# A two-block fp32 network on one core: FFN groups loaded two ahead, gates one tile ahead, last sums of the layer norms on TensorE

## The chip, the cores and the metric

The kernel runs on one core of one Trainium2 chip. The metric is the device time of one execution in microseconds (us). The kernel before ran three times; its time is the median of the three. One further execution was taken by the hardware profiler, and every row shown below is from that one.

## What is computed

The input x has 1024 positions of 1024 channels, float32, and passes two blocks. Cut to what the change touches:

```python
def first_block(x, ...):
    x = x + mix @ w_out                      # mix: gated delta rule and spatial gating of rms_norm(x)
    h = rms_norm(x, norm_ffn)                # norm1
    ff = square(relu(h @ w_ff1))             # 1024 -> 4096
    x = x + ff @ w_ff2                       # 4096 -> 1024
    return rms_norm(x, norm_final)           # norm2
def second_block(x, ...):
    u, h, c_gate, b_gate, gate_a, gate_b = split(x @ w_in + b_in)
    y_a = glu(gelu(s5_ssm(u))) @ w_ssm_out   # S5: diagonal complex state, 32 groups
    y_b = (b_gate * conv(c_gate * h)) @ w_conv_out
    merged = sigmoid(gate_a) * y_a + sigmoid(gate_b) * y_b
    x = layer_norm(ALPHA * x + merged @ w_o, ln1_g, ln1_b)
    hid = silu(x @ w_gate) * (x @ w_up)      # 1024 -> 2816
    return layer_norm(ALPHA * x + hid @ w_down, ln2_g, ln2_b)
```

## The kernel before, in words

Channels lie on the 128 partitions and positions on the free axis, so an activation is eight tiles of 128x1024, each handled in two halves (`HS`) of 512 positions. Every fp32 operand of a product is split into a high and a low part (`split`, L342 to L344: ACT writes the high part, DVE or POOL subtracts it to get the low one), and a product is three passes, high times high, high times low and low times high (`mm`, L1316 to L1325). Weights come as pieces of 128x512 (256 KB): SP issues the load into one of three buffers `wr` (L620), then ACT writes `wh` and DVE or POOL `wl`.

**Order of work.** TensorE's order is the program's. The order on DVE, ACT, POOL and SP is set by a scheduler that simulates the program with estimated times; `K.late` keeps one instruction at its place in the program. Tiles come from pools that are opened and closed like a stack. `arena` opens one small pool for each numbered slot of 4 KB per partition, `sl` takes a tile in a slot, and a tile that reuses memory waits for the last readers of what lay there.

**Stages.** After `w_out` comes norm1 with `Forms` (L85 to L158): for the two big FFN products the kernel keeps seven combinations b11, b21, t1, t2, t3, t4, b22 of the activation's quarters, so that a unit (`sunit`, L1378) needs seven block products (`sprod`) where a direct form needs eight. `first` splits b11 and b21 as the tiles become final; `rest` makes the others, beginning with the four differences `ts` (t1, L125). `ffn1` runs 16 units, writes its 32 result tiles to DRAM (`ffd`), and reads them back in eight groups of four tiles (`load`, L1446); `unpack` splits a group into `fh` and `fl` (16 splits in two groups, 8 in one), and `down` multiplies it with `w_ff2` for the eight output tiles and adds to `res` (L1526). Between these products the generator `side` prepares the S5 tables (`s5_prep`): small DVE operations on 128x32 tiles, then four TensorE transposes (L1693). `arena()` (a local function of `mixers`) first closes the pools of ffn1's forms and opens the slots anew; only then are the S5 tiles taken.

In the second block, `merge` makes for each of eight output tiles two gate products (evacuated by a sigmoid), then the products with `w_conv_out` and `w_ssm_out`, and merges them. The merged tiles are split into `mh` and `ml`, `w_o` is multiplied (`wo`, `wo2`), and `ln_tail` makes the layer norm, first the sums of the first half (`N[0]`), then of the second (`N[1]`), which end under the first units of the second FFN. The layer norm (`Ln`) first subtracts a shift, the mean over the first four tiles (`shift_stat`, `shift_bc`, `sub`), then sums x and x*x tile by tile on DVE (`add`: L212 the sum `s`, L204 the sum `q` of the squares that ACT makes at L203) and adds over the 128 partitions with products of one column against ones (`colsums`, L1290; `stat`). The second FFN has 22 units, and `w_down` in five groups of tiles, read back like ffn1's; `ln2` is the last layer norm, and its end is the end of the program.

Of the kernel before, what the change touches and what calls it, by code (L numbers as in the profile page):

```python
# [16 lines left out]
P = 128  # L17
# [67 lines left out]
class Forms:  # L85
# [30 lines left out]
    def rest(self):  # L116
# [4 lines left out]
        for j, ((b11, b12), (b21, b22)) in enumerate(q):  # L121
            t = K.sl(self.slots["t4"] + j, "ts")
            t1, t2 = t[:, :HF], t[:, HF:]
            raw.append((t1, t2))
            V.tensor_tensor(t1, b12, b11, op=su)  # L125
            if self.gain:
                n.append(K.tmp("acc"))
                A.activation(n[j], b22, AF.Copy, scale=K.vec(self.gain, j + 4))
                V.scalar_tensor_tensor(t2, t1, self.neg[:, j:j + 1], n[j], op0=m, op1=ad)
            else:  # L130
                V.tensor_tensor(t2, b22, t1, op=su)
            self.split("t2", j, t2)
            yield
# [27 lines left out]
class Ln:  # L161
# [115 lines left out]
class Kern:  # L277
# [1176 lines left out]

    def finish(self, us, src, base):
# [9 lines left out]
        self.unpack(t)  # L1465
        for _ in u:
            pass
        return t

    def ffn1(self, F, res, sums, w0, arena):  # L1470
# [43 lines left out]
        for _ in rest:  # L1514
            pass
        ffs = [None] * 8
        base = (8, 16, 0, 8, 16, 0, 8, 16)
        ffs[0] = self.finish(us, ffd[:4], base[0])
        side = arena()
# [259 lines left out]
    def block2(self, y, N1, yd):  # L1779
# [172 lines left out]
        def sig(b, store):  # L1952
# [4 lines left out]
            return ev  # L1957
        for d in range(KD):
            for b, c in ((16, 2048), (24, 3072)):
                self.unit((W, c + d * P, y, sig(b, d)))  # L1960
            m = self.sl(mslot[d], "m")

            def evb(h, ps):
                V.tensor_tensor(m[:, self.HS[h]], ps, st["s", 24, h], op=M_)

            def eva(h, ps):
                t = st["s", 16, h]
                V.tensor_tensor(t, ps, t, op=M_)
# [4 lines left out]
        mg = [(self.sl(d, "mh", F32R), self.sl(8 + d, "ml", F32R)) for d in range(KD)]  # L1973
        for h in range(2):
            sl = self.HS[h]
            for d in range(KD):
                self.split(mg[d][0][:, sl], mg[d][1][:, sl], md[d][:, sl], (V, G)[d % 2])
        self.mark("wo")
        res = []
        for d in range(KD):  # L1980
            x = self.sl(100 + d, "res")
            dma(x, yd[d])
            res.append(x)
        def wo(d, hs):
            w = self.wts(I["w_o_2"], 0, d * P, KD)
            for h in hs:
# [16 lines left out]
        wl = []  # L2003
        for u in range(4):
            o = []
            for i in (12, 13) if u == 0 else (14, 15) if u == 1 else (2 * u + 4, 2 * u + 5):
                t = self.sl(X + i, "wx", F32R).rearrange("p (e t c) -> p e t c", e=2, t=4)
                o.append((t[:, 0], t[:, 1]))
            wl.append(self.left(I[("w_gate_2", "w_up_2")[u % 2]], u // 2 * 2 * P, o))
        self.ln_tail(N, wo, lambda d: self.wts(I["w_o_2"], 0, d * P, KD), wo2, pre, 2, 6)  # L2010
# [25 lines left out]
        for i in range(ahead):  # L2036
            next(us[i])
            next(us[i])
            for d in {1: (0, 1, 2, 3), 2: (4, 5, 6, 7)}.get(i, ()):
                n1.fin(d)  # L2040
            if i > 1:
                for _ in range(2):
# [3 lines left out]
        groups = [(0, 4), (4, 4), (8, 4), (12, 4), (16, 6)]  # L2046
        base = (X, 0, 8, X + 8, 0)

        def take(k, ts):
            for i, t in enumerate(ts):  # L2050
                hid[groups[k][0] + i] = t
        take(0, self.finish(us, hd[:4], base[0]))

        def down(f0, n, d, hs):
            w = self.wts(I["w_down_2"], f0 * P, d * P, n)
            for h in hs:
                sl = self.HS[h]
                ps = self.mm(w, [hid[f0 + k] for k in range(n)], sl)
                if f0 == 0:
# [3 lines left out]
        for k, (f0, n) in enumerate(groups[:-1]):  # L2063
            f1, m = groups[k + 1]
            ts = self.load(hd[f1:f1 + m], base[k + 1])
            self.unpack(ts)
            take(k + 1, ts)
            for d in range(KD):
                down(f0, n, d, (0, 1))
        self.mark("ln2")  # L2070
# [12 lines left out]
        def last(d, n, w, at):  # L2083
            sl = n.sl
            ps = self.mm(w, [hid[16 + k] for k in range(6)], sl, at)
            V.tensor_tensor(res[d][:, sl], ps, res[d][:, sl], op=Ad)
        N = self.ln_tail(N, lambda d, hs: down(16, 6, d, hs), wlast, last, pre2, 1, 4, True)
        N.stat()
        N.bc()
        for d in range(KD):  # L2090
            N.fin(d)

    def ln_tail(self, N, prod, wts, prod2, pre, ka, kb, cut=False):

# [11 lines left out]
        def bc(n):  # L2106
# [3 lines left out]
            for d in range(4):  # L2110
                n.sub(d)
        w = None
        parts = [N[0]]
        for k in range(2):
            if k == 1:
                parts.append(N[1])
            for d in range(4, KD):
# [5 lines left out]
                if k == 0:  # L2123
                    at = {4: {ka: stat, kb: lambda: bc(N[0])}, 5: {kb: lambda: bc(N[1])}}.get(d, {})
                else:
# [66 lines left out]
    def build(self):  # L2192
        tc, I = self.tc, self.I
        with ExitStack() as top:
# [12 lines left out]
            with tc.manual_schedule(engines={mybir.EngineType.PE}):  # L2207
                def arena():
                    self.fes.close()
                    self.arena(es, 8, 16)  # L2210
                    return self.s5_prep()
# [135 lines left out]
```

## Time and profile before

| | us |
|---|---|
| three runs: lowest, median, highest | 2880.91, 2884.34, 2886.09 |
| profiled execution, its own time | 2889.28 |
| its span in the profile | 2887.5 |
| TensorE (PE) busy | 2652.8 |
| DVE, POOL, ACT busy | 1569.5, 1092.4, 1005.8 |
| mean granted TensorE clock, share of 2.4 GHz | 0.952 |

The span runs from the first to the last instruction of the profile; the execution's own time has 1.8 us more, outside it, and lies 4.9 us over the median of the three runs. PEclk 1.00 is 2.4 GHz, 0.50 is 1.2 GHz. A row "[3.63 <-ACT fh L343]" says that the engine stood 3.63 us before this instruction and that the ACT instruction writing `fh` at line 343 released it. SPq rows are DMA issues. A row with x4 stands for four like instructions in a run.

### The profile page before, as it was taken

The page shows a single profiled execution, that of the slowest core. Times are in us where ns is not written, and L with a number is a line of the kernel's source. Part 1 is how long each engine was busy: PE and PEld are TensorE (multiplying, and loading weights), DVE is VectorE, ACT ScalarE, POOL GpSimd, SP SyncE. Part 2 cuts the span into 40 slices and gives each one's busy share as a digit, 9 for nine tenths or more (in the row PEclk, how much of TensorE's full clock was granted, in tenths as well). Part 3 has the DMA queues.
Part 4 walks back from the last instruction along what each step waited for, and adds up shares of the span by engine and source line. Part 5 has one row for each costly group of instructions (what it writes and reads, how often), then busy time and mean ns, then how long its engine had stood idle before and what let it go on. Part 6 is the DMA issues. An engine that isn't in the chain of part 4 may idle for free.

```text
span 2887.5 us, 39623 instructions
## 1 busy us (share of the span) xinstructions
PE 2652.8 (92%) x15032; PEld 2126.5 (74%) x15032; DVE 1569.5 (54%) x2585; ACT 1005.8 (35%) x1664; POOL 1092.4 (38%) x1041
## 2 busy tenths in 40 slices
PE   7776999799899999699999999999887999999996
PEld 5555676576678888588787887888666888888885
DVE  7799658864585545555554344100488444345337
ACT  4543442433354444212224224111244333343213
POOL 5765434332215331089804332333333433333220
PEclk9888998899989999899999999999998999999998
DMA  3332143221224334445425342111321322234311
GB/s 98 93 82 70 42 126 83 67 103 51 83 85 132 105 117 150 136 142 161 142 85 191 108 142 67 48 48 48 128 66 44 95 88 81 85 108 144 95 44 58
DMA packets 297118, 277.18 MB, mean 96 GB/s; under 512 B 26240, under 2 KB 248576, under 8 KB 296672
## 3 DMA queue, kind: packets, MB, share of 16 engines
q1 hardware_dynamic: 296928, 274.66, 30.8%
q8 instruction: 118, 1.93, 0.3%
q14 instruction: 72, 0.59, 0.1%
HBM read 210.23 MB, written 64.10 MB: 95 GB/s over the span
## 4 chain that ended last, share of the span: by engine, by line
PE 68%; DVE 18%; issue 4%; POOL 4%; DMA 3%; ACT 2%; SPq 1%; ACTq 0%; DVEq 0%; POOLq 0%
PE mm L1325 31%; PE mm L1376 24%; PE mm L636 5%; DVE stp L982 2%; DVE h L984 2%; PE wu L800 2%; DVE cy L789 1%; DMA fl<-ffd 1%; PE ob L800 1%; DVE acc L204 1%; DVE xl L424 1%; DVE fl L344 1%; PE cp L800 1%; DVE fbgkq L789 1%; DVE res L240 1%
## 5 line engine op out<-in xcount | busy, mean ns | idle before, releaser
L344 POOL TENSOR_TENSOR wl<-wr,wh 128x512 fp32r<-128x512 f32 (+1 forms) x261 | 346.0, 1326 | 855.2 <-ACT wh L343 772.7
L343 ACT ACTIVATE wh<-wr 128x512 fp32r<-128x512 f32 (+1 forms) x410 | 251.0, 614 | 801.1 <-PE mm L1325 460.4
L1376 PE MATMUL mm<-t,wh 128*128 128x512 f32 x1216 | 376.8, 391 | 9.8 <-DVE t L344 7.9
L1325 PE MATMUL mm<-fh,wh 128*128 128x512 f32 x816 | 321.5, 394 | 6.4 <-ACT fh L343 3.6
L1325 PE MATMUL mm<-fl,wh 128*128 128x512 f32 x816 | 320.1, 392 | 0.3 <-DVE fl L344 0.2
L1325 PE MATMUL mm<-fh,wl 128*128 128x512 f32 x816 | 319.3, 391 | 0.0
L1376 PEld LDWEIGHTS mm<-t,wh 128*128 128x128 f32 x1216 | 229.1, 189 | 59.1 <-DVE t L344 8.2
L1376 PE MATMUL mm<-b,wh 128*128 128x512 f32 x848 | 266.1, 394 | 6.0 <-DVE b L110 4.8
L1376 PE MATMUL mm<-t,wl 128*128 128x512 f32 x608 | 237.3, 390 | 0.0
L1325 PE MATMUL mm<-yh,wh 128*128 128x512 f32 x512 | 201.9, 394 | 0.0
L1325 PE MATMUL mm<-yl,wh 128*128 128x512 f32 x512 | 200.4, 391 | 1.0 <-DVE yl L344 1.0
L1325 PE MATMUL mm<-yh,wl 128*128 128x512 f32 x512 | 200.2, 391 | 0.0
L636 PE MATMUL mm<-xh,wh 128*128 128x512 f32 (+1 forms) x400 | 173.1, 433 | 24.4 <-ACT rows L851 7.2
L1376 PEld LDWEIGHTS mm<-b,wh 128*128 128x128 f32 x848 | 161.0, 190 | 42.5 <-DVE b L110 6.9
L1325 PEld LDWEIGHTS mm<-fh,wh 128*128 128x128 f32 x816 | 154.4, 189 | 41.4 <-ACT fh L343 7.8
L1407 POOL TENSOR_TENSOR ws<-wr 128x512 f32<-128x512 f32 x38 | 58.8, 1548 | 329.1 <-DVE wl L344 209.8
L344 DVE TENSOR_TENSOR wl<-wr,wh 128x512 fp32r<-128x512 f32 x149 | 110.6, 743 | 129.8 <-ACT wh L343 129.7
L1325 PEld LDWEIGHTS mm<-fl,wh 128*128 128x128 f32 x816 | 154.3, 189 | 33.8 <-DVE fl L344 2.0
L1325 PEld LDWEIGHTS mm<-fh,wl 128*128 128x128 f32 x816 | 154.4, 189 | 32.1
L636 PE MATMUL mm<-xl,wh 128*128 128x512 f32 (+1 forms) x400 | 171.2, 428 | 4.1 <-DVE xl L424 4.0
L344 DVE TENSOR_TENSOR wl<-ws,wh 128x512 fp32r<-128x512 f32 x152 | 113.4, 747 | 105.9 <-ACT wh L343 105.9
L636 PE MATMUL mm<-xh,wl 128*128 128x512 f32 (+1 forms) x400 | 169.6, 424 | 0.0
(504 smaller groups left out, 5448.6 us busy)
## 6 DMA issues: line engine op xcount, KB each, us to landing
wr<-in_w_in SPq DMA_DIRECT2D x112, 256.0 KB
wr<-in_w_ff SPq DMA_DIRECT2D x82, 256.0 KB
wr<-in_w_ff SPq DMA_DIRECT2D x32, 512.0 KB
fl<-ffd SPq DMA_DIRECT2D x32, 512.0 KB
wr<-in_w_gate SPq DMA_DIRECT2D x22, 512.0 KB
wr<-in_w_up SPq DMA_DIRECT2D x22, 512.0 KB
fl<-hd SPq DMA_DIRECT2D x22, 512.0 KB
wr<-in_w_down SPq DMA_DIRECT2D x40, 256.0 KB
```

The costliest lines, as they stand in the source:

```text
L204: K.V.tensor_tensor(self.q, self.q, t, op=ALU.add)
L240: K.V.tensor_tensor(r, r, self.rb, op=ALU.mult)
L343: self.A.activation(hi, src, AF.Copy)
L344: (lo_eng or self.V).tensor_tensor(lo, src, hi.bitcast(F32), op=ALU.subtract)
L636: self.T.matmul(ps, a[:, t, :], b[:, sl], start=(first and j == 0), stop=(last and j == 2))
L789: V.scalar_tensor_tensor(y[:, a:b], raw[:, a + o:b + o], cw[:, k:k + 1], y[:, a:b], op0=ALU.mult, op1=ALU.add)
L800: self.T.matmul(out(s), lhsT(s), rhs(s), start=start, stop=stop)
L982: V.tensor_tensor(tm, X3[:, :, 0:j, j:j + 1].to_broadcast([P, 2, j, n]), T3[:, :, j:j + 1, m:16].to_broadcast([P, 2, j, n]), op=ALU.mult)
L984: V.tensor_tensor(T3[:, :, 0:j, m:16], T3[:, :, 0:j, m:16], tm, op=ALU.subtract)
L1325: self.T.matmul(ps, a, b[:, sl], start=(start and k + j == 0), stop=(stop and k == n - 1 and j == 2))
L1376: self.T.matmul(ps, a[:, k, :], b, start=(start and k + j == 0), stop=(k == 3 and j == 2), skip_group_check=True)
L1407: G.tensor_tensor(s1, r21, r22, op=add)
```

## The change

It has six parts, each a change of order, of memory or of the engine that does a sum; what is computed stays the same.

1. `Forms.rest`: the difference t1 is kept at its place in the program (`K.late`).
2. ffn1: the slots of the forms are renumbered, so that the slots of FFN groups 0 and 1 (8 to 23) belong to an arena that stays open; only slots 24 to 27 and the pool `nf` are closed before the S5 preparation. `finish` loads groups 0 and 1, and the loop loads group g + 2.
3. merge: the gate products of tile d + 1 are put ahead of the products of tile d; the tiles 0 to 6 are split after the last gate product; the addition into m and all splits go to DVE (POOL made the low parts of every second tile before). Of the first `w_gate` and `w_up` pieces, one pair is now issued with each of the first four `w_o` tiles, where all four pairs stood ahead.
4. `Ln.add`: the last tile of eight gets no DVE addition; `stat` sums it on TensorE, 16 one-column products where 8 were.
5. Second FFN: groups two ahead, as in ffn1; the second half's `fin` in the order j, j + 4.
6. ln2: the products of group 3 for the output tiles 4 to 7 (`mid`) come after those of group 4 for tiles 0 to 3, and the shift of both halves is made among them.

```diff
@@ class Forms, rest
-            V.tensor_tensor(t1, b12, b11, op=su)
+            K.late(V.tensor_tensor(t1, b12, b11, op=su))
@@ class Ln, add
+        if d == KD - 1:
+            t = K.tmp("t")[:, :r.shape[-1]]
+            K.A.activation(t, r, AF.Square)
+            self.end = r, t
+            return
         self.sq(d)
@@ class Ln, stat
-        K.colsums(st[:, :n], self.s)
-        K.colsums(st[:, n:], self.q)
+        for e, xs in enumerate(zip((self.s, self.q), self.end)):
+            for i, x in enumerate(xs):
+                for k in range(n):
+                    K.T.matmul(st[:, e * n + k:e * n + k + 1], x[:, k * P:(k + 1) * P], K.ones[:, 0:1],
+                               start=e + i + k == 0, stop=i == 1, skip_group_check=True)
@@ finish
-        t = self.load(src, base)
+        ts = [self.load(*l) for l in loads]
@@ ffn1
-        ffs[0] = self.finish(us, ffd[:4], base[0])
+        src = [(ffd[4 * g:4 * g + 4], base[g]) for g in range(8)]
+        ffs = self.finish(us, src[:2])
         side = arena()
...
-            ffs[g + 1] = self.load(ffd[4 * g + 4:4 * g + 8], base[g + 1])
+            if g < 6:
+                ffs.append(self.load(*src[g + 2]))
@@ merge
-        for d in range(KD):
+        gates(0)
+        for d in range(KD):
+            if d + 1 < KD:
+                gates(d + 1)
+            else:
+                for e in range(KD - 1):
+                    part(e)
...
-                G.tensor_tensor(m[:, self.HS[h]], m[:, self.HS[h]], t, op=Ad)
+                V.tensor_tensor(m[:, self.HS[h]], m[:, self.HS[h]], ga[h], op=Ad)
...
-                self.split(mg[d][0][:, sl], mg[d][1][:, sl], md[d][:, sl], (V, G)[d % 2])
+        part(KD - 1)
@@ wo
+            ahead_w(d)
             w = self.wts(I["w_o_2"], 0, d * P, KD)
...
-        F = Forms(self, (X, X + 4, 4, 8, 0, X + 8, 12), res)
+        F = Forms(self, (X, X + 4, 0, 4, 8, X + 8, 12), res)
@@ ffn2, last groups
+        for k in range(4):
+            if k < 2:
+                ts.append(self.load(*src[k + 2]))
+            elif k == 2:
+                ts.append(self.load(hd[16:20], 0))
+            else:
+                ts[4] += self.load(hd[20:], 8)
+            self.unpack(ts[k + 1])
+            for d in range(KD if k < 3 else 4):
+                down(k, d, (0, 1))
@@ ln_tail
+        if mid:
+            for d in range(4, KD):
+                mid(d)
+                (stat, lambda: bc(N[0]), lambda: bc(N[1]), lambda: None)[d - 4]()
@@ mixers
-            self.arena(self.fes, 8, 20)
+            self.arena(es, 8, 16)
+            self.arena(self.fes, 24, 4)
...
-            F = Forms(self, (8, 12, 24, 20, 16, 4, 0), res, "norm_ffn")
+            F = Forms(self, (8, 12, 16, 20, 24, 4, 0), res, "norm_ffn")
```

**The order on DVE in norm1.** Rows are instructions in DVE's order, with their line. `b` is a form b11, b21 or b22, `ts` the raw difference t1, `res` the last addition of a product with `w_out`. Before:

```order
L2165 TENSOR_TENSOR res<-mm,res 128x512
L344 TENSOR_TENSOR wl<-wr,wh 128x512
L2165 TENSOR_TENSOR res<-mm,res 128x512
L125 TENSOR_TENSOR ts<-res 128x512 x2
L2187 TENSOR_TENSOR t<-t 128x512
L125 TENSOR_TENSOR ts<-res 128x512 x2
L344 TENSOR_TENSOR wl<-wr,wh 128x512
L110 SCALAR_TENSOR_TENSOR b_6958<-res,vecs,b_6958 128x512
L129 SCALAR_TENSOR_TENSOR ts<-ts,neg,acc 128x512
L110 SCALAR_TENSOR_TENSOR b_6994<-res,vecs,b_6994 128x512
L129 SCALAR_TENSOR_TENSOR ts<-ts,neg,acc 128x512
L110 SCALAR_TENSOR_TENSOR b_7032<-res,vecs,b_7032 128x512
```

And with the change, from the same last additions on:

```order
L110 SCALAR_TENSOR_TENSOR b_7211<-res,vecs,b_7211 128x512
L353 TENSOR_TENSOR wl<-wr,wh 128x512
L2194 TENSOR_TENSOR res<-mm,res 128x512
L353 TENSOR_TENSOR t_7618<-cb,t_7618 128x512
L353 TENSOR_TENSOR wl<-wr,wh 128x512
L2194 TENSOR_TENSOR res<-mm,res 128x512
L353 TENSOR_TENSOR wl<-wr,wh 128x512
L110 SCALAR_TENSOR_TENSOR b_7255<-res,vecs,b_7255 128x512
L2216 TENSOR_TENSOR t<-t 128x512 x2
L141 SCALAR_TENSOR_TENSOR cb<-res,neg,acc 128x512
L110 SCALAR_TENSOR_TENSOR b_7635<-res,vecs,b_7635 128x512
L353 TENSOR_TENSOR wl<-wr,wh 128x512
```

Before, the four differences stood ahead of eight splits of `b` (L110) that the first products read; with the change seven of these eight have gone ahead of the last addition, one (b_7255) is left behind it with one of b22, and the first difference comes eleven rows below the last one shown.

**The order on SP at the end of ffn1.** `ffd` numbers count the FFN's result tiles; in the rows of before 7285 is the first, so 7289 to 7292 are group 1 and 7297 the first of group 3. Before:

```order
L1483 DMA ffd_7315<-acc 128x512
L1483 DMA ffd_7316<-t 128x512
L620 DMA wr<-in_w_ff 128x4x128 x8
L1446 DMA fl<-ffd_7289 128x1024
L1446 DMA fl<-ffd_7290 128x1024
L1446 DMA fl<-ffd_7291 128x1024
L1446 DMA fl<-ffd_7292 128x1024
L1604 DMA s5t_9946<-in_s_b 128x512
L1604 DMA s5t_9947<-in_s_b 128x512
L1606 DMA s5t_9951<-in_c_i 16x16
L1606 DMA s5t_9952<-in_s_d 16x32
L1614 DMA d_m<-s5t_9955 4096x1x128
```

With the change 7288 is the first, so 7292 to 7295 are group 1 and 7296 to 7299 group 2:

```order
L1455 DMA fl<-ffd_7291 128x1024
L1455 DMA fl<-ffd_7292 128x1024
L629 DMA wr<-in_w_ff 128x4x128
L1455 DMA fl<-ffd_7293 128x1024
L1492 DMA ffd_7318<-t 128x512
L1455 DMA fl<-ffd_7294 128x1024
L1455 DMA fl<-ffd_7295 128x1024
L629 DMA wr<-in_w_ff 128x4x128
L1455 DMA fl<-ffd_7296 128x1024
L1455 DMA fl<-ffd_7297 128x1024
L1455 DMA fl<-ffd_7298 128x1024
L629 DMA wr<-in_w_ff 128x4x128
```

Group 1 has moved from behind eight pieces of `w_ff2` to just behind group 0; the S5 loads and the write of `d_m` now stand ahead of the last ten pieces that come before group 3.

**The order on SP at the product with `w_o`.** Before:

```order
L1982 DMA res<-yd_13049 128x1024
L1982 DMA res<-yd_13050 128x1024
L1982 DMA res<-yd_13051 128x1024
L620 DMA wr<-in_w_up 128x4x128
L620 DMA wr<-in_w_gate 128x4x128 x2
L620 DMA wr<-in_w_up 128x4x128 x2
L620 DMA wr<-in_w_o 128x4x128 x24
```

With the change:

```order
L629 DMA wr<-in_w_conv_out 128x4x128
L629 DMA wr<-in_w_ssm_out 128x4x128
L629 DMA wr<-in_w_gate 128x4x128 x2
L629 DMA wr<-in_w_o 128x4x128 x2
L629 DMA wr<-in_w_up 128x4x128 x2
L629 DMA wr<-in_w_o 128x4x128
L2003 DMA res<-yd_13045 128x1024
```

The first two pieces of `w_o` now stand behind one pair of `w_gate` pieces, where four pairs and the loads of `res` stood ahead of them.

## Rows read from the trace of the kernel before

**Rows 1.** page, part 1, PE: busy us (share of the span) xinstructions.

```profile
PE 2652.8 (92%) x15032; PEld 2126.5 (74%) x15032; DVE 1569.5 (54%) x2585; ACT 1005.8 (35%) x1664; POOL 1092.4 (38%) x1041
```

**Rows 2.** windows, columns: PE, PEld, DVE, ACT, POOL busy; PEclk; DMA share; GB/s.

```profile
1137.00:1182.00 45.00, 43.87 (x194) 36.01 (x192) 22.08 (x38) 9.98 (x18) 0.00 (x0) 1.00 0.30 97
1182.00:1211.10 29.10, 8.09 (x24) 4.90 (x24) 26.69 (x129) 11.79 (x22) 0.00 (x0) 0.68 0.75 257
2600.00:2830.00 230.00, 229.93 (x1019) 189.62 (x1018) 96.91 (x136) 51.30 (x92) 58.42 (x47) 1.00 0.27 87
```

**Rows 3.** timeline, PE, norm1; in brackets: idle before it and releaser.

```profile
819.61 0.79 PE L1376 MATMUL mm<-b,wh 128*128 128x512 f32 x1 [3.44 <-DVE b L110]
...
822.26 0.79 PE L1376 MATMUL mm<-b,wh 128*128 128x512 f32 x1 [1.01 <-DVE b L110]
```

**Rows 4.** timeline of DVE, norm1, beside it.

```profile
815.20 1.28 DVE L125 TENSOR_TENSOR ts<-res 128x512 f32<-128x512 f32 x2
...
817.01 1.28 DVE L125 TENSOR_TENSOR ts<-res 128x512 f32<-128x512 f32 x2
```

**Rows 5.** timeline, PE, ffn1 and S5 preparation.

```profile
1184.50 0.49 PE L1325 MATMUL mm<-fh,wh 128*128 128x512 f32 x1 [3.63 <-ACT fh L343]
...
1211.14 1.22 PE L1693 MATMUL mm<-ident,s5t 128*128 128x128 f32 x4 [18.22 <-DVE s5t L1686]
```

**Rows 6.** timeline of SP's queue, ffn1, DMA issues.

```profile
1142.21 34.94 SPq L620 DMA_DIRECT2D wr<-in_w_ff  x8
1180.22 1.76 SPq L1446 DMA_DIRECT2D fl<-ffd  x4
...
1185.09 8.91 SPq L620 DMA_DIRECT2D wr<-in_w_ff  x2
```

**Rows 7.** groups of DVE, 1182 to 1211 us, the largest.

```profile
L344 DVE TENSOR_TENSOR fl<-fl,fh 128x512 fp32r<-128x512 f32 x16 | 10.8, 683 | 0.6 <-ACT fh L343 0.6
```

**Rows 8.** timeline of PE, a later FFN group.

```profile
1421.17 0.66 PE L1325 MATMUL mm<-fh,wh 128*128 128x512 f32 x1 [2.81 <-DVE res L1526]
```

**Rows 9.** timeline of PE, the first product with w_o.

```profile
2052.39 0.80 PE L1325 MATMUL mm<-mh,wh 128*128 128x512 f32 x1 [14.00 <-ACT wh L343]
```

**Rows 10.** timeline of SP's queue before it.

```profile
2048.28 11.10 SPq L620 DMA_DIRECT2D wr<-in_w_o  x7
```

**Rows 11.** timeline, PE, first layer norm.

```profile
2133.46 3.54 PE L1290 MATMUL mm<-ones,acc 128*128 128x1 f32 x16 [5.12 <-DVE acc L212]
...
2169.70 1.84 PE L1290 MATMUL mm<-ones,acc 128*128 128x1 f32 x8 [7.79 <-DVE acc L212]
2174.16 1.86 PE L1290 MATMUL mm<-ones,acc 128*128 128x1 f32 x8 [2.62 <-DVE acc L204]
...
2212.12 0.80 PE L1376 MATMUL mm<-t,wh 128*128 128x512 f32 x1 [7.93 <-DVE t L344]
```

**Rows 12.** timeline, DVE, the first layer norm's last sums.

```profile
2166.00 1.75 DVE L204 TENSOR_TENSOR acc<-acc,t 128x512 f32<-128x512 f32 x1
...
2172.36 1.75 DVE L204 TENSOR_TENSOR acc<-acc,t 128x512 f32<-128x512 f32 x1
```

**Rows 13.** timeline of PE, last layer norm, the column sums.

```profile
2839.06 1.02 PE L1290 MATMUL mm<-ones,acc 128*128 128x1 f32 x8 [1.10 <-ACT t L203]
2841.76 1.86 PE L1290 MATMUL mm<-ones,acc 128*128 128x1 f32 x8 [1.68 <-DVE acc L204]
...
2864.11 2.68 PE L1290 MATMUL mm<-ones,acc 128*128 128x1 f32 x16 [3.48 <-DVE acc L212]
```

**Rows 14.** windows at low clock: PE busy, PEclk, DMA share, GB/s.

```profile
817.20:834.20 17.00, 13.24 (x37) 0.50 0.05 15
1196.20:1216.40 20.20, 5.26 (x14) 0.50 0.35 131
2042.60:2056.10 13.50, 3.58 (x8) 0.50 0.59 178
2841.30:2847.90 6.60, 6.14 (x19) 0.50 0.00 1
```

More of the change, by code (lines that the diff above doesn't have):

```diff
@@ L1453, in unpack, with finish @@
                 self.split(fh[:, sl], fl[:, sl], fl[:, sl].bitcast(F32))
-    def finish(self, us, src, base):
+    def finish(self, us, loads):
         for u in us[:-1]:
@@ L1462, in finish @@
         next(u); next(u)
-        t = self.load(src, base)
+        ts = [self.load(*l) for l in loads]
         next(u)
-        self.unpack(t)
+        self.unpack(ts[0])
         for _ in u:
             pass
-        return t
+        return ts
     def ffn1(self, F, res, sums, w0, arena):
@@ L1515, in ffn1 @@
             pass
-        ffs = [None] * 8
         base = (8, 16, 0, 8, 16, 0, 8, 16)
-        ffs[0] = self.finish(us, ffd[:4], base[0])
+        src = [(ffd[4 * g:4 * g + 4], base[g]) for g in range(8)]
+        ffs = self.finish(us, src[:2])
         side = arena()
@@ L1957, in sig, with gates, part @@
             return ev
-        for d in range(KD):
+        def gates(d):
             for b, c in ((16, 2048), (24, 3072)):
                 self.unit((W, c + d * P, y, sig(b, d)))
+            st["g", d] = [[st["s", b, h] for h in range(2)] for b in (16, 24)]
+        def part(d):
+            sl = self.HS
+            mg.append((self.sl(d, "mh", F32R), self.sl(8 + d, "ml", F32R)))
+            for h in range(2):
+                self.split(mg[d][0][:, sl[h]], mg[d][1][:, sl[h]], md[d][:, sl[h]])
+        mg = []
+        gates(0)
[5 more added lines that the diff above has]
+                    part(e)
             m = self.sl(mslot[d], "m")
+            ga, gb = st["g", d]
             def evb(h, ps):
-                V.tensor_tensor(m[:, self.HS[h]], ps, st["s", 24, h], op=M_)
+                V.tensor_tensor(m[:, self.HS[h]], ps, gb[h], op=M_)
             def eva(h, ps):
-                t = st["s", 16, h]
-                V.tensor_tensor(t, ps, t, op=M_)
-                G.tensor_tensor(m[:, self.HS[h]], m[:, self.HS[h]], t, op=Ad)
+                V.tensor_tensor(ga[h], ps, ga[h], op=M_)
+                V.tensor_tensor(m[:, self.HS[h]], m[:, self.HS[h]], ga[h], op=Ad)
             self.unit((I["w_conv_out_2"], d * P, bz, evb))
@@ L1972, in block2 @@
             md.append(m)
[L1973 to L1976, printed above, removed]
-                self.split(mg[d][0][:, sl], mg[d][1][:, sl], md[d][:, sl], (V, G)[d % 2])
+        part(KD - 1)
         self.mark("wo")
@@ L1983, in block2, with ahead_w @@
             res.append(x)
+        wl = []
+        def ahead_w(u):
+            o = []
+            for i in (12, 13) if u == 0 else (14, 15) if u == 1 else (2 * u + 4, 2 * u + 5):
+                t = self.sl(X + i, "wx", F32R).rearrange("p (e t c) -> p e t c", e=2, t=4)
+                o.append((t[:, 0], t[:, 1]))
+            wl.append(self.left(I[("w_gate_2", "w_up_2")[u % 2]], u // 2 * 2 * P, o))
         def wo(d, hs):
+            ahead_w(d)
             w = self.wts(I["w_o_2"], 0, d * P, KD)
@@ L1998, in block2 @@
         N = [Ln(self, res, h, "ln1_g", "ln1_b") for h in range(2)]
-        F = Forms(self, (X, X + 4, 4, 8, 0, X + 8, 12), res)
+        F = Forms(self, (X, X + 4, 0, 4, 8, X + 8, 12), res)
         for n in N:
             n.out = F
[L2003 to L2009, printed above, removed]
         self.ln_tail(N, wo, lambda d: self.wts(I["w_o_2"], 0, d * P, KD), wo2, pre, 2, 6)
@@ L2038, in block2 @@
             next(us[i])
-            for d in {1: (0, 1, 2, 3), 2: (4, 5, 6, 7)}.get(i, ()):
-                n1.fin(d)
-            if i > 1:
+            for j in {1: (0, 1), 2: (2, 3)}.get(i, ()):
+                n1.fin(j)
+                n1.fin(j + 4)
+                next(rest)
+            if i > 2:
                 for _ in range(2):
@@ L2047, in block2, with down @@
         base = (X, 0, 8, X + 8, 0)
[L2049 to L2055, printed above, removed]
+        src = [(hd[f:f + n], b) for (f, n), b in zip(groups, base)]
+        ts = self.finish(us, src[:2])
+        def down(k, d, hs, w=None, at={}):
+            f0, n = groups[k]
+            w = w or self.wts(I["w_down_2"], f0 * P, d * P, n)
             for h in hs:
                 sl = self.HS[h]
-                ps = self.mm(w, [hid[f0 + k] for k in range(n)], sl)
-                if f0 == 0:
+                ps = self.mm(w, ts[k], sl, at)
+                if k == 0:
                     V.scalar_tensor_tensor(res[d][:, sl], res[d][:, sl], ALPHA, ps, op0=M_, op1=Ad)
@@ L2062, in down @@
                     V.tensor_tensor(res[d][:, sl], ps, res[d][:, sl], op=Ad)
[L2063 to L2069, printed above, removed]
+        for k in range(4):
[8 more added lines that the diff above has]
+                down(k, d, (0, 1))
         self.mark("ln2")
@@ L2081, in wlast, with ln_tail @@
             return [(hi[:, t, :], lo[:, t, :]) for t in range(6)]
[L2083 to L2089, printed above, removed]
+        n = self.ln_tail(N, lambda d, hs: down(4, d, hs), wlast, lambda d, n, w, at: down(4, d, (n.h,), w, at), pre2, 1, 4,
+                         True, lambda d: down(3, d, (0, 1)))
+        n.stat()
+        n.bc()
         for d in range(KD):
-            N.fin(d)
-    def ln_tail(self, N, prod, wts, prod2, pre, ka, kb, cut=False):
+            n.fin(d)
+    def ln_tail(self, N, prod, wts, prod2, pre, ka, kb, cut=False, mid=None):
         for d in range(4):
@@ L2123, in ln_tail @@
                 if k == 0:
-                    at = {4: {ka: stat, kb: lambda: bc(N[0])}, 5: {kb: lambda: bc(N[1])}}.get(d, {})
+                    at = {} if mid else {4: {ka: stat, kb: lambda: bc(N[0])}, 5: {kb: lambda: bc(N[1])}}.get(d, {})
                 else:
@@ L2209, in arena @@
                     self.fes.close()
-                    self.arena(es, 8, 16)
                     return self.s5_prep()
```

## The prediction

> **What bounds the kernel now.** I read the page first. TensorE (PE) is busy 92% of the span [rows 1], so a gain can only come from the remaining gaps or from faster multiplying. The windows then show where there are gaps: none in the second FFN's last groups, where PE is busy for 229.93 of 230 us at the full clock [rows 2], but 8.09 of 29.10 us busy between 1182 and 1211 us. The timeline of PE gives each gap its length and releaser; after 800 us nearly all of it lies in six places: norm1 [rows 3], ffn1 with the S5 preparation [rows 5], a later FFN group [rows 8], the first product with `w_o` [rows 9], and the two layer norms [rows 11, 13]. Last come the windows at low clock: behind most waits PEclk is 0.50, the 1.2 GHz level [rows 14]. At 2.4 GHz a matmul of 512 columns takes 229.93/1019 = 0.226 us [rows 2]; at the low level the 37 in 13.24 us, 16 of them one-column sums, and the 14 in 5.26 us give 0.36 to 0.38 [rows 14], partly because short gaps and cheap ones lie among them. I charge 0.20 us for each 512-column matmul at the low level, from 0.226 to about 0.43, twice 0.226. A wait thus costs its length and this surcharge.
>
> **Norm1.** The reader is to see what DVE does while PE waits: four differences, 1.28 us for two and again 1.28 us for two [rows 4], ahead of the splits of `b` that release PE after 3.44 and 1.01 us [rows 3]. The order with the change has seven of the eight splits ahead of the last addition. Waits of 4.45 us go, and with them 21 wide matmuls at the low level, 37 less 16 sums, 21 x 0.20 = 4.2 us [rows 14]; together 8.6 us. What is late next: the lows of t2, now behind the differences. I count 45 DVE operations of 0.68 us and 12 small ones of 0.16 between the last addition and the last t2, 32.5 us, while PE has 120 wide matmuls (27.1 us), 16 sums and 4 broadcasts, some 31 us. That is a draw, and a new wait may be 0 to 4 us, with a surcharge as much again at worst. Bounds: 0.6 to 8.6. I take **6**, nearer the upper end, as the scheduler puts the t2 it can wherever DVE is free.
>
> **ffn1 and S5.** PE waits 3.63 us for the first high part of group 1 and 18.22 us for the S5 tables [rows 5]. SP shows why: eight `w_ff2` pieces go out one by one from 1142.21, and only at 1180.22 group 1 and then the S5 loads [rows 6]; all wait for the old pools, which PE reads until then. With the change group 1 stands just behind group 0, and the S5 tiles wait only for slots 24 to 27 and `nf`, last used by ffn1's last unit, which is over when the pieces of group 0's products are issued from 1142.21 on. DVE then has to hide the tables. In the 29.10 us of the wait it is busy 26.69 [rows 2], 10.8 of it splits of two groups [rows 7], so the tables are at most 15.9 us, or 13 without four other wide operations of 0.68. In 1137 to 1182 us DVE is busy 22.08 of 45 us [rows 2], which leaves 22.9; until PE reaches the transposes, 24 matmuls later, another 5.4. The load is 13 to 15.9 and 5.4 for the eight splits of group 1: 18.4 to 21.3 of 28.3 us. It fits by 7 us, if small operations don't queue badly. The write of `d_m` holds SP: the two weight pieces behind it take 8.91 us to issue [rows 6]. With the change eight pieces stand there that are issued 3 to 4 products ahead of use (5.44 us each, 24 matmuls), so 16 us or more cover it; were that cover gone, 8.9 us would show once. The gain: 3.63 + 18.22, plus 14 matmuls at the low level [rows 14], four of them transposes (some 2.4): 24.3 at most; 8 if the tables end 16 us later than needed, all of DVE's 15.9. I take **23**, near the upper end, as the count leaves 7 us.
>
> **The later group.** The 2.81 us at 1421 [rows 8] come of DVE standing behind splits whose loads were issued late; a group earlier they are on chip. Bounds 0 and 2.81 plus 1.6, if eight matmuls follow at the low level as behind `w_o`, 4.4. I take **3**. In the second FFN the same edit has nothing to hide [rows 2]: 0.
>
> **Merge and `w_o`.** PE waits 14.00 us for the first high part of `w_o` [rows 9], whose load is issued only at 2048.28 [rows 10], 9.9 us after PE stopped (2052.39 - 14.00 = 2038.39), behind the four pairs. With the change two pieces of `w_o` stand behind one pair, and the last gate product comes 21.8 us (96 matmuls) earlier, so that twelve splits of tiles 0 to 5 run under the last two products. Only tile 7's chain (an addition, a split, about 2.8 us at 0.68 each) is left, and it is wanted as the last of eight in a 5.44 us product. POOL's additions move to DVE: 16 x 0.68 = 11 us over eight tiles, beside PE at 100%. The gain: 14.00 and 8 matmuls at the low level (1.6) [rows 14] = 15.6 at most; at least 2, if the buffers come free only at PE's end, as before. I take **15**.
>
> **Column sums.** Each of four sums loses two DVE additions and gets 16 rows more (8 products; the profile shows two rows for each). The 16 rows take 3.54 us in the first layer norm [rows 11] and 2.68 in the last [rows 13], 8 rows 1.02 at best: 0.13 to 0.22 us a row, 2.0 to 3.5 us for 16. The Trainium skill ("TensorE: Matmul & The Clock Gate", section "Back-to-back issue gap") puts a floor of about 25 ns under the start of one matmul to the next however few its columns. By that floor, an estimate, 16 rows would take 0.4 us and the four sums together gain some 8 us more than I forecast; the trace does not agree, with 0.13 us at best, and I go by the rows.
> - First layer norm, first half: the wait of 5.12 ends with L212 [rows 11]. The sums of tile 6 end some 2 us before those of tile 7, and 16 more rows take 2.0 to 3.5 of it back: -1 to +2.5, I take **1**.
> - Second half: the waits of 7.79 and 2.62 [rows 11] end with tile 7's two sums. With the change the last DVE addition is tile 6's, which ends at 2167.75, against 2174.11 for tile 7's [rows 12]. Sixteen rows of `q` at the low level follow, 3.6 us: end 2171.4, where the sums now end at 2176.0. Gain **4.6**; 1.7 if the three weight splits slip in, 6 if the clock stays up. The 7.93 us at 2212 [rows 11] stay: DVE is what PE waits for there, and the order leaves 42 of the 43 operations ahead of that split.
> - Last layer norm, first half: 1.10 + 1.68 [rows 13], and 11 wide matmuls at the low level, 19 less 8 sums (2.2) [rows 14], with the shift's 16 DVE operations now under group 3's products. Less 2.0 for the rows: 0 to 5, I take **3**.
> - Its second half ends the program: two additions less (1.4), 16 rows more (2.0 to 3.5), of which `s` can run earlier: -2 to +1, **0**.
>
> **The sum.** 6 + 23 + 3 + 15 + 1 + 4.6 + 3 = 55.6 us from the profiled execution's own 2889.28: 2833.7. That execution lies 4.9 us over the median of the three runs; taken at the same distance the median is 2828.8, so **2829**. All upper bounds together are 67.4 us, median 2817; all lower ones about 9, median 2875.
>
> **Rivals.**
> 1. *The S5 tables are still late.* DVE is in order, and the 109 small operations (129 less 16 splits and four others) wait for each other and stand between evacuations. For it: DVE had 26.69 of 29.10 us of work there [rows 2]. Against it: 7 us to spare. If half the wait stays, 9 us and its surcharge 3 go back: 2841.
> 2. *`w_o` is still late.* The `w_gate` pieces are split into slots that the merge's last products may hold, and ACT would stand there ahead of `w_o`. For it: the order on SP still has one pair ahead of `w_o`. Against it: the first pair lies where tiles 4 and 5 were, which are split 20 us earlier. It costs 14: 2843.
> 3. *Group 1 and S5 wait for the pools as before*, that is, the change does not do what it says. Then 23 and part of the 3 are lost: 2853. Against it: the order on SP, and that the arena for slots 8 to 23 is open from the start.
> 4. *Slower.* In ffn1's down products SP carries 4 MB of groups and the 2 MB of `d_m` at once with 256 KB pieces of `w_ff2`. If pieces came late in each of the 64 products from there on, PE would wait once per product and fall to 1.2 GHz behind each wait, as behind the waits of [rows 14]. It decides from 55.6/64 = 0.9 us per product; at 1.2 us the time is 2829 + 77 = 2906. Against it: PE is at 43.87 of 45 us and the DMA share is 0.30 in 1137 to 1182 [rows 2], and half the traffic would still fit.
>
> **Chances.** Forecast, all parts within their bounds: 0.66. Rival 1: 0.12; rival 2: 0.09; rival 3: 0.06; rival 4: 0.03; several small new waits, time within 0.2% of before, 0.04. A measurement can tell about 0.2%, 6 us. Faster: 0.66 + 0.12 + 0.09 + 0.06 = 0.93; same 0.04; slower 0.03. The range of 2813 to 2857 takes in rivals 1 to 3; it leaves out rival 4 and the 0.04 above, and some 0.10 of forecast and rivals at either edge, where bounds add up.
>
> **What would show it.** Right: SP issues group 1 before 1135 us; no wait over 2 us before the transposes; `w_o` loads before the merge's end and PE without a gap there; at low clock no window after 1140 to 1540; 32 rows in each sum. Norm1 wrong: a wait for `t` at L1385 near 845 us. Rival 1: a wait for `s5t`; rival 2: ACT waiting ahead of `wx`. The forecast is wrong if new waits of over 20 us stand where none were, above all on DVE in 1140 to 1190 us.

## The result, and the profile after

The changed kernel takes 2832.64 us (median of 4 runs, 2831.41 to 2834.16) where before takes 2885.22 (median of 4 runs as well, one more than ahead of the prediction; 2880.91 to 2887.94): a ratio of 0.9819, 95% interval 0.9802 to 0.9836. The forecast was 2829 in 2813 to 2857.

PE's row of the page, part 1, of the kernel after:

```profile
PE 2649.6 (94%) x15096; PEld 2126.8 (75%) x15096; DVE 1576.1 (56%) x2601; ACT 1006.6 (36%) x1664; POOL 1074.6 (38%) x1017
```

Against [rows 1], PE works as long as before (2652.8) in a span that is 57.1 us shorter (2887.5 to 2830.4): waits went, not work. The second view is the windows of ffn1 and the S5 preparation after, columns as in [rows 2]:

```profile
1137.00:1182.00 45.00, 45.00 (x200) 37.28 (x199) 39.90 (x157) 13.32 (x27) 0.00 (x0) 1.00 0.59 182
1182.00:1211.10 29.10, 29.10 (x136) 24.26 (x135) 15.85 (x25) 9.00 (x21) 6.83 (x9) 1.00 0.38 116
```

DVE now does in 1137 to 1182 what it did in the wait: 39.90 us busy against 22.08, PE has no gap, and PEclk is 1.00 in both windows.

Since PE runs the same products in both kernels, but for the sums, I read the trace at eight of them and compare the stretches between (us; the product that ends a stretch is the same in both, and the last stretch ends with ACT's last instruction):

| stretch | before | after | less by | forecast |
|---|---|---|---|---|
| start to the last product with `w_out` | 814.2 | 814.4 | -0.2 | 0 |
| norm1 and the 16 units of ffn1 | 323.0 | 321.2 | 1.8 | 6 |
| first down products, S5 tables | 83.9 | 56.2 | 27.7 | 23 |
| later groups | 301.7 | 301.8 | -0.1 | 3 |
| norm2, u, conv, S5 | 228.1 | 227.4 | 0.7 | 0 |
| glu, merge, first product with `w_o` | 312.1 | 292.8 | 19.3 | 15 |
| first layer norm, first half | 79.8 | 77.4 | 2.4 | 1 |
| second half, units of the second FFN | 470.9 | 466.9 | 4.0 | 4.6 |
| its down products, last layer norm, end | 270.6 | 269.2 | 1.4 | 3 |

The waits that are left, from the timeline of PE after (norm1, a later group, the two layer norms):

```profile
852.27 0.80 PE L1385 MATMUL mm<-t,wh 128*128 128x512 f32 x1 [3.31 <-DVE t L353]
...
856.88 0.79 PE L1385 MATMUL mm<-t,wh 128*128 128x512 f32 x1 [2.96 <-DVE t L353]
...
1382.78 0.50 PE L1334 MATMUL mm<-fh,wh 128*128 128x512 f32 x1 [1.80 <-DVE res L1535]
...
2080.81 1.05 PE L227 MATMUL mm<-ones,res 128*128 128x1 f32 x8 [0.69 <-DVE res L2026]
2082.49 1.05 PE L227 MATMUL mm<-ones,acc 128*128 128x1 f32 x8 [0.63 <-DVE acc L204]
...
2111.01 1.02 PE L227 MATMUL mm<-ones,acc 128*128 128x1 f32 x8 [0.97 <-DVE acc L218]
...
2115.94 1.87 PE L227 MATMUL mm<-ones,acc 128*128 128x1 f32 x8 [3.01 <-DVE acc L204]
...
2154.88 0.79 PE L1385 MATMUL mm<-t,wh 128*128 128x512 f32 x1 [6.37 <-DVE t L353]
...
2804.92 1.05 PE L227 MATMUL mm<-ones,acc 128*128 128x1 f32 x8 [2.27 <-DVE acc L218]
2805.84 1.03 PE L227 MATMUL mm<-ones,res 128*128 128x1 f32 x8
2806.73 1.44 PE L227 MATMUL mm<-ones,acc 128*128 128x1 f32 x8
2808.03 1.85 PE L227 MATMUL mm<-ones,t 128*128 128x1 f32 x8
```

The waits before the b products [rows 3], before the transposes [rows 5] and before `w_o` [rows 9] have no successor. Two are new, 3.31 and 2.96 us before t2 in norm1. The sums of the first layer norm begin after 0.69 and 0.97 us where they waited 5.12 and 7.79 [rows 11], but now PE stands 3.01 us inside them; the 32 rows at the end of the program take 4.96 us (2804.92 to 2809.88), where 16 took 2.68 [rows 13].

### The profile page after: what moved, and what is told of

Read it like the earlier page. It is cut to its first block, busy times and chain, and to the rows that moved or that the text cites. A ratio compares the mean times of both kernels' runs of the same rounds, so it can differ in the third digit from the quotient of the medians.

```text
span 2830.4 us, 39715 instructions
## 1 busy us (share of the span) xinstructions
PE 2649.6 (94%) x15096; PEld 2126.8 (75%) x15096; DVE 1576.1 (56%) x2601; ACT 1006.6 (36%) x1664; POOL 1074.6 (38%) x1017
## 4 chain that ended last, share of the span: by engine, by line
PE 75%; DVE 17%; issue 3%; DMA 2%; ACT 2%; POOL 1%; SPq 0%; ACTq 0%; POOLq 0%; DVEq 0%
PE mm L1334 38%; PE mm L1385 25%; PE mm L645 5%; DVE h L993 2%; DVE stp L991 2%; PE wu L809 2%; DVE cy L798 1%; DVE fbgkq L798 1%; DVE xl L433 1%; DVE res L249 1%; PE ob L809 1%; PE gram L809 1%; PE cp L809 1%; PE mm L227 1%; DMA ca<-rd 0%
## 5 line engine op out<-in xcount | busy, mean ns | idle before, releaser
L353 POOL TENSOR_TENSOR wl<-wr,wh 128x512 fp32r<-128x512 f32 (+1 forms) x261 | 352.6, 1352 | 871.9 <-ACT wh L352 781.9
L1416 POOL TENSOR_TENSOR ws<-wr 128x512 f32<-128x512 f32 x38 | 65.1, 1712 | 316.3 <-DVE wl L353 216.3
```

What stands on the lines that cost most here:

```text
L353: (lo_eng or self.V).tensor_tensor(lo, src, hi.bitcast(F32), op=ALU.subtract)
L1416: G.tensor_tensor(s1, r21, r22, op=add)
```

## The experiments

Each kernel is the changed one with one edit (`slots_old` and `ws_dve2` have two, `best` three), timed beside the kernel before on the same chip, and profiled once. The part ahead of norm1, which no edit touches, took 809.3 to 817.0 us in these profiles, so medians of neighbours a few us apart don't decide; the stretches do. They scatter too: over the changed kernel and those whose edit lies elsewhere, norm1 with its units took 318.9 to 321.5 us, the later groups 300.4 to 302.4, glu, merge and the first product with `w_o` 292.4 to 296.3, the first half of the first layer norm 77.4 to 79.7, its second half with the units 464.5 to 466.9, the end 268.5 to 270.9. Only what lies outside these is read as an effect.

**What freed the S5 tables: memory or the order of the loads?** Two kernels. In the first, loads go back to one group ahead in the program, slots as changed:

```diff
-        ffs = self.finish(us, src[:2])
+        ffs = self.finish(us, src[:1])
-            if g < 6:
-                ffs.append(self.load(*src[g + 2]))
+            ffs.append(self.load(*src[g + 1]))
```

> The slots stay as changed, but ffn1 loads its groups one ahead, as before. Theory: the S5 preparation waited for memory, so the freed slots alone remove the wait of 18 us before the transposes; group 1 is issued a little later but no longer behind a pool, at most 4 us come back: 2833 to 2837. Rival: it is the early issue of group 1 that counts; then PE waits some 4 us for its high part and the splits push the S5 tables behind the transposes again: 2845 to 2860.

Measured: 2829.77 us, ratio to before 0.9801 (0.9786 to 0.9815); the S5 stretch 56.2 us, as after. SP's queue, DMA issues, of this kernel:

```profile
1114.37 0.32 SPq L1455 DMA_DIRECT2D fl<-ffd  x1
...
1115.73 4.40 SPq L1455 DMA_DIRECT2D fl<-ffd  x4
...
1122.11 0.43 SPq L1455 DMA_DIRECT2D fl<-ffd  x1
...
1123.55 0.84 SPq L1455 DMA_DIRECT2D fl<-ffd  x2
...
1126.59 3.04 SPq L1455 DMA_DIRECT2D fl<-ffd  x3
...
1130.67 0.32 SPq L1455 DMA_DIRECT2D fl<-ffd  x1
```

These are twelve group loads, three groups, before 1131 us, in the same order as after: the scheduler issues a load when its slot is free, wherever it stands in the program. The rival falls, and of the theory's 4 us at most nothing came back: loading two ahead is worth nothing here. In the second, the slots go back too:

```diff
-            self.arena(es, 8, 16)
-            self.arena(self.fes, 24, 4)
+            self.arena(self.fes, 8, 20)
-            F = Forms(self, (8, 12, 16, 20, 24, 4, 0), res, "norm_ffn")
+            F = Forms(self, (8, 12, 24, 20, 16, 4, 0), res, "norm_ffn")
...
+                    self.arena(es, 8, 16)
```

> ffn1 as before (old slots, groups one ahead), all else as changed. Theory: the freed slots alone carry the S5 gain, so the waits of 3.6 and 18.2 us and the low clock behind them are back, 27.6 us from the first down product to behind the transposes: 2857 to 2860. Rival: part of the S5 gain came of the other parts (other order on DVE and SP): under 20 us.

Measured: 2861.76 us, ratio 0.9913 (0.9897 to 0.9930); the S5 stretch is 83.4 us, 27.2 more than after. PE's timeline has the old waits again:

```profile
1183.86 0.80 PE L1334 MATMUL mm<-fh,wh 128*128 128x512 f32 x1 [3.61 <-ACT fh L352]
...
1211.04 1.22 PE L1702 MATMUL mm<-ident,s5t 128*128 128x128 f32 x4 [17.72 <-DVE s5t L1695]
```

The theory holds: the memory carries the whole gain, and rival 3's mechanism is what the edit brings back. (Norm1, whose forms lie in their old slots again in this kernel, takes 324.7 us, 3.5 more than after; that is a second loss and not part of the 27.2.)

**What freed `w_o`: SP's order or the gates?** In one kernel the gate products go back to just ahead of their tile:

```diff
-        gates(0)
         for d in range(KD):
-            if d + 1 < KD:
-                gates(d + 1)
-            else:
+            gates(d)
+            if d + 1 == KD:
                 for e in range(KD - 1):
                     part(e)
```

> Gate products in the old order (tile d just ahead of its own products), splits of tiles 0 to 6 after the last gate product and w_o pieces between the pairs as changed. Theory: the place of the w_o pieces on SP is what removed the 14 us; the splits still have the last two products of 10.9 us as cover, so 0 to 1 us comes back: 2833. Rival: the cover by the gate product moved ahead is needed, tile 6 or the weights are late: 2838 to 2847.

Measured: 2829.34 us, ratio 0.9801 (0.9782 to 0.9820), the merge stretch 292.9 us against 292.8. In the other the four pairs stand ahead of `w_o`:

```diff
+        for u in range(4):
+            ahead_w(u)
         def wo(d, hs):
-            ahead_w(d)
```

> Gates one tile ahead as changed, but all four pairs of w_gate and w_up pieces ahead of w_o, as before. Theory (SP's order decides): the w_o load is again issued behind pieces whose buffers come free only when the merge ends, PE stands 10 to 14 us before the first product with w_o and runs on at the low clock: 2844 to 2849. Rival: with the gates ahead the three buffers turn over early enough and nothing comes back: 2833.

Measured: 2838.27 us, ratio 0.9842 (0.9821 to 0.9862), the merge stretch 304.0, 11.2 more. PE's timeline in this kernel:

```profile
2009.47 0.79 PE L1334 MATMUL mm<-mh,wh 128*128 128x512 f32 x1 [8.15 <-ACT wh L352]
```

And SP's queue, the issues of the pieces and of the `w_o` load:

```profile
1997.80 5.26 SPq L629 DMA_DIRECT2D wr<-in_w_up  x2
2003.28 7.88 SPq L629 DMA_DIRECT2D wr<-in_w_o  x4
```

PE waits 8.15 us, for `wh`, whose load is issued at 2003.28 behind the last `up` pieces. After, it is issued at 1990.19 and PE goes on without a gap; SP's queue in the kernel after:

```profile
1990.19 0.92 SPq L629 DMA_DIRECT2D wr<-in_w_o  x2
```

The time rose less than expected, the stretch by the lower end of it. Gates a tile ahead are worth nothing here, the pieces' place on SP 11 us. In both kernels the splits of the merged tiles stay on DVE and behind the last gate product, as changed; that was not undone, and what the remaining 5 of that stage's 16.3 us came from stays open.

**Norm1.** The difference t1 back at the scheduler's choice (`K.late` removed):

> Part 1 alone undone (t1 no longer kept at its place). Theory: in norm1 DVE is the limit from 815 to 858 us, so the change only moved a wait from the b products to the t products; undone, the waits of 3.4 and 1.0 us before the b products are back, those of 3.3 and 3.0 before the t products are gone, and the first down product starts 1.6 us later: 2834. Rival A: keeping t1 late gives the 6 us of the forecast and the new waits come of something else: 2839. Rival B: it does harm, without it the time falls: 2829.

Measured: 2839.24 us, ratio 0.9835 (0.9819 to 0.9851); norm1's stretch 326.9 us, 5.7 more than after and 3.9 more than before. PE's timeline:

```profile
815.92 3.13 PE L2200 MATMUL mm<-ones,t 128*128 128x1 f32 x16 [2.41 <-DVE t L2216]
...
844.16 3.61 PE L1311 MATMUL mm<-dg,ones 128*128 128x512 f32 x4 [9.20 <-DVE dg L1304]
```

The size is rival A's, but the waits are neither theory's: none before b or t, but 9.20 us before the broadcast of the norm's scale, whose small DVE operations the differences had pushed back. So the wait moves with DVE's order. Not all of it is order, though. DVE's timeline in this kernel, two of the small operations:

```profile
836.95 1.23 DVE L347 SCALAR_TENSOR_TENSOR qy<-qt,qy 128x8 f32<-128x8 f32 x1
838.21 0.17 DVE L345 TENSOR_TENSOR qt<-qy 128x8 f32<-128x8 f32 x1
```

Four of them took 1.12 to 1.23 us where the others take about 0.17, some 4 of the 9.20 us, and each of the four lay beside an operation on POOL, whose first here runs from 836.86 to 838.16. Why does DVE not keep up? DVE's timeline of the kernel after:

```profile
839.18 0.68 DVE L125 TENSOR_TENSOR ts<-res 128x512 f32<-128x512 f32 x1
839.78 1.77 DVE L129 SCALAR_TENSOR_TENSOR ts<-ts,neg,acc 128x512 f32<-128x512 f32 x1
841.48 1.77 DVE L353 TENSOR_TENSOR t<-cb,t 128x512 fp32r<-128x512 f32 x1
843.18 1.78 DVE L110 SCALAR_TENSOR_TENSOR t<-ts,vecs,t 128x512 fp32r<-128x512 f32 x1
```

POOL's timeline of the same stretch:

```profile
836.16 4.84 POOL L1416 TENSOR_TENSOR ws<-wr 128x512 f32<-128x512 f32 x1 [60.05 <-DMA wr<-in_w_ff]
841.08 1.62 POOL L1417 TENSOR_TENSOR ws<-ws,wr 128x512 f32<-128x512 f32 x1
842.67 1.74 POOL L1428 TENSOR_TENSOR ws<-wr 128x512 f32<-128x512 f32 x1
844.37 1.74 POOL L1434 TENSOR_TENSOR ws<-wr,ws 128x512 f32<-128x512 f32 x1
```

An addition or split of 128x512 takes 0.68 us until 839.18 and 1.77 from 839.78 on, one for each POOL operation of 1.6 to 1.7; POOL's own first took 4.84 beside DVE's of 0.68, where the shortest of this line's 38 takes 1.27 and the median 1.62. Of the 24 such DVE operations from 836 to 860, nine took over 1 us (mean 1.73) and each lay beside a POOL one. The Trainium skill ("SBUF — State Buffer", section "SBUF: two separate sides") says that a DVE instruction with two SBUF inputs contends with a GpSimd instruction that reads SBUF, and that whoever comes first holds the shared ports for its whole instruction; the trace agrees, in turns of about 1.7 us. A test of it: the weight sums of the first two units go to DVE, more work on the engine that is late.

```diff
-        G.tensor_tensor(s1, r21, r22, op=add)
+        we.tensor_tensor(s1, r21, r22, op=add)      # s2, s3, s4 alike; we = V in units 0 and 1, else G
```

> The weight sums (s1 to s4) of the first two units of ffn1 go from POOL to DVE: 8 more operations of 0.68 us on the engine that PE waits for. Theory: DVE operations that ran beside POOL's took 1.75 us in place of 0.68, nine of them between 840 and 858 us, 9.6 us lost; without POOL DVE ends earlier by 9.6 - 5.4 = 4 us, the waits of 3.3 and 3.0 us before the t products shrink to under 3 together, and the time falls to 2827 to 2830. Rival: DVE is simply full, 5.4 us more work on it lengthens the waits: 2836 to 2840.

Measured: 2822.03 us, ratio 0.9771 (0.9755 to 0.9787); norm1's stretch 314.0, 7.2 less than after. PE's timeline before t2 in this kernel:

```profile
851.97 0.50 PE L1385 MATMUL mm<-t,wh 128*128 128x512 f32 x1 [1.40 <-DVE t L353]
```

And DVE's:

```profile
840.20 0.68 DVE L125 TENSOR_TENSOR ts<-res 128x512 f32<-128x512 f32 x1
840.80 0.74 DVE L129 SCALAR_TENSOR_TENSOR ts<-ts,neg,acc 128x512 f32<-128x512 f32 x1
841.46 0.68 DVE L353 TENSOR_TENSOR t<-cb,t 128x512 fp32r<-128x512 f32 x1
842.07 0.68 DVE L1418 TENSOR_TENSOR ws<-ws,wr 128x512 f32<-128x512 f32 x1
842.67 0.69 DVE L1429 TENSOR_TENSOR ws<-wr 128x512 f32<-128x512 f32 x1
```

One wait of 1.40 us is left of 6.27, and the sums themselves (L1418, L1429) take 0.68. Of the 37 operations on DVE from 836 to 860 us one takes over 1 us, beside POOL's only operation there (849.07, 1.69 us), and the split that ends the wait stands right behind it:

```profile
849.53 1.78 DVE L154 SCALAR_TENSOR_TENSOR cb<-res,vecs,ts 128x512 f32<-128x512 f32 x1
851.23 0.68 DVE L353 TENSOR_TENSOR t<-ts,t 128x512 fp32r<-128x512 f32 x1
```

The theory holds, with more than it counted (7.2 us in norm1 for 4), and the rival falls. The same in the second FFN's first two units:

> As ws_dve, and the same in the second FFN's first two units, beside the second half's sums. Theory: the slow DVE operations there (1.75 us) shorten as well, the waits of 3.0 us before the sums and 6.4 us before t2 shrink, 2 to 5 us more than ws_dve: 2822 to 2828. Rival: the additional work on DVE, which PE waits for at t2, costs 5.4 us there: 2832 to 2835.

Measured: 2823.32 us, ratio 0.9775 (0.9758 to 0.9792); the second half of the first layer norm and the units take 461.8 us (466.9 after), norm1 314.1. That stretch is 5 us shorter than after, but the median does not show it, and `best` below, which has the same edit, takes 464.1 us there, where kernels without it take 464.5 to 466.9. The 6.37 us before t2 became three waits of 6.0 together. The rival's loss did not come, but a gain in the second FFN is not shown.

**The sums.** On DVE again (`add` and `stat` as before):

> Part 4 undone: the last tile of each layer norm sum is added on DVE again, 8 one-column products per sum. Theory, from the stages of the two profiles: first layer norm loses 2 us in the first half and 3.5 in the second, the last layer norm gains about 1 at the very end: 2837. Rival: the saved time is taken up by the wait for t2 behind it, 2833 to 2834.

Measured: 2832.55 us, ratio 0.9812 (0.9797 to 0.9827). The median is the rival's, but the part ahead of norm1 took 5.1 us less in this profile and norm1 2.3. Of the stretches, the second half with its units agrees with the theory, 472.3 (466.9 after), and so does the end, 267.4 (269.2); the first half, 78.6 (77.4), lies within the scatter. PE's timeline again has 4.52, 7.80 and 2.61 us before the sums:

```profile
2075.25 3.54 PE L1290 MATMUL mm<-ones,acc 128*128 128x1 f32 x16 [4.52 <-DVE acc L212]
...
2111.48 1.84 PE L1290 MATMUL mm<-ones,acc 128*128 128x1 f32 x8 [7.80 <-DVE acc L212]
2115.93 1.87 PE L1290 MATMUL mm<-ones,acc 128*128 128x1 f32 x8 [2.61 <-DVE acc L204]
```

The shift of the last layer norm back inside the last products (`mid` removed):

> Part 6 undone: all of group 3 ahead of group 4 and the shift inside the last products, as before; sums on PE. Theory: the wait before the first half's sums went because the last DVE additions went, so the shift's place is worth under 1 us: 2833. Rival: the 16 DVE operations of the shift, put among group 3's products, are what removed the waits of 1.1 and 1.7 us and the low clock after them; 2 to 4 us come back: 2835 to 2837.

Measured: 2830.3 us, ratio 0.9801 (0.9787 to 0.9816); the end takes 270.0 us against 269.2, within what the stretch scatters. The theory's under 1 us stands; it was not tried with the sums on DVE.

**A version that beats both.** `ws_dve2`, and the last layer norm's sums on DVE:

```diff
-        if d == KD - 1:
+        if d == KD - 1 and self.g == "ln1_g":
```

> ws_dve2 with the last layer norm's sums on DVE again (the first layer norm's stay on TensorE). Theory from the stages: 7 us in norm1 and 4 at the second FFN's first units as in ws_dve2, and 1.5 us at the program's end, where 16 rows of one column on TensorE cost more than two DVE additions: 12 to 13 us under the changed kernel on the same chip, 2819 to 2822. Rival: the end's gain does not come without the first half's, 10 to 11 us.

Measured: 2818.05 us (5 runs), ratio to before 0.9757 (0.9739 to 0.9775). The changed kernel beside it on the same chip:

> The changed kernel once more, unchanged, beside the two others on the same chip: 2830 to 2835; its stages show how far a stage scatters when nothing in it differs (theory: norm1 and the later FFN group by 2 us, the first layer norm and the merge by less than 1; rival: the differences of 1 to 2 us read from single stages are scatter everywhere).

Measured: 2829.27 us, ratio 0.9805 (0.9784 to 0.9825). The two intervals don't meet; `best` is 11.2 us faster, between the theory's 12 to 13 and the rival's 10 to 11. Against the profile of the kernel beside it, norm1 takes 7.7 us less and the end 4.3, but the second FFN's units only 0.8, where the theory counted 4. Its end takes 266.2 us, 3 less than after. PE's timeline of the last layer norm's sums:

```profile
2771.63 1.84 PE L227 MATMUL mm<-ones,acc 128*128 128x1 f32 x16
...
2793.81 2.36 PE L227 MATMUL mm<-ones,acc 128*128 128x1 f32 x16 [3.48 <-DVE acc L218]
```

The wait of 3.48 us is back, but with 16 rows in 2.36 us that makes 5.84, where after has a wait of 2.27 and 32 rows in 4.96 (2804.92 to 2809.88), 7.23. As for scatter: between the two profiles of the same kernel, norm1, S5, later groups, merge and first half differ by 0.3 us at most, the second half with its units by 2.0, the end by 1.2. The theory had put the 2 us into norm1 and the later group. Kernels with an edit elsewhere scatter more, by 2 to 4 us in each of these stretches but S5 (56.2 in all of them), so differences of 1 to 2 us are not read as effects, except where the waits in the timeline name them.

## Why the prediction was right

The sum of the stretches is 57 us against 55.6 forecast; on the profiled execution's own time, span plus 1.8 us, that is 2832.2 against 2833.7. That they lie so close is in part luck: two terms that came out 4.7 and 4.3 us larger than forecast (S5, `w_o`) stand against two that came out 4.2 and 3.1 smaller (norm1, the later group), and the part ahead of norm1, which scatters by 8 us, took the same time in both profiles. The 3.6 us between 2829 and 2832.64 come of the last step: I took the median 4.9 us below the profiled execution, as before, and after, the two agree. Point by point:

- **S5: right, too small.** 27.7 for 23, beyond my upper bound of 24.3. The term left out the matmuls at the low level between 1184.50 and the transposes: the 24 that should take 5.4 us took from 1184.50 to 1192.92, 8.4 [rows 5, with 1211.14 - 18.22]. DVE's added load, 39.90 - 22.08 = 17.8 us, is near the 18.4 to 21.3 counted, and the tables were ready. Rivals 1 and 3 did not come; that the extra loads do nothing I had not seen.
- **`w_o`: right, and for 11 of 16 us by the reason given first, the place on SP.** The stretch has 19.3, of which some 3 lie in glu: two waits there of 0.99 and 1.47 with low clock behind them became one of 1.24, in stages that the change does not touch; `no_late` and `slots_old`, where the stretch is 3 longer again, show it as scatter. The rest is 16.3 for 15. Rival 2 did not come. The second reason, the gates ahead as cover for twelve splits, fell with `gates_old`: they give nothing. They also come 48 matmuls, 10.9 us, earlier than before and not 21.8: the last gate product now ends 21.6 us ahead of `w_o` (1983.85 to 2005.45), where 10.9 us of products lay behind it.
- **Norm1: the step that failed.** The waits before b went as forecast, 4.45 and the low clock behind them; the new wait before t2 was counted as "45 DVE operations of 0.68 us" and so as a draw of 0 to 4. Nine of them took 1.73 beside POOL, 9 x 1.05 = 9.5 us, and PE waited 6.27 and ran at the low clock after. The forecast of 6 became 1.8, or 1.5 to 4.1 if the scatter of this stretch is counted in.
- **The later group: failed.** 3 was forecast, 0 came: the wait at 1421 is gone, one of 1.80 at 1382.78 stands in its place, again on DVE behind splits whose loads SP issues late (from 1376.15; ACT waits 11.88 us for them). PEclk is 0.50 from 1384 to 1387 us, so the sign that 1140 to 1540 would be free of low clock did not come either. That loads would come "a group earlier" was wrong, as `one_ahead` shows for the first groups; the queue itself was not tried.
- **Sums.** 2.4 for 1, 4.0 for 4.6, 1.4 for 3, but only the second is clear of the scatter: kernels with the same sums take 77.4 to 79.7 us in the first half (before 79.8) and 268.5 to 270.9 at the end (before 270.6). The 7.93 us before t2, which were to stay, became 6.37. Eight rows take 1.02 to 1.05 us at best in [rows 13] and after, 0.13 us a row. The estimate of 0.4 us for 16 rows, by the floor of about 25 ns in the Trainium skill ("TensorE: Matmul & The Clock Gate", section "Back-to-back issue gap"), thus did not come. That `q` keeps PE waiting 3.01 us inside the sum was not forecast.
- **Rival 4** did not come: DMA share 0.59 in 1137 to 1182 (0.30 before), and PE without a gap.

## What to carry to other kernels

A wait behind a pool is a wait for memory: find out which tiles' last readers hold it, and free those slots early; where a scheduler places the loads, moving the load call alone moved nothing. In a queue, work that is not needed soon must not stand ahead of what is, and PE's order above it may be without effect. Count DVE's time beside POOL's work, not alone: in a stretch that DVE limits, taking work off POOL onto DVE gained 7 us.

## What was not expected of the hardware

DVE operations on 128x512 with two operands in SBUF take 0.68 us alone and 1.73 beside POOL, one for each POOL operation, and small ones on 128x8 take 1.12 to 1.23 in place of 0.17. A POOL operation that takes 1.27 at its shortest took 4.84 beside six of 0.68 on DVE. Each POOL operation cost DVE about 1.05 us, more than the 0.68 that the same sum takes on DVE itself.
